# A decoder trunk on one core: MLP weights split once and kept in DRAM, relu and square through SBUF

## The chip, the core and the metric

One NeuronCore of a Trainium2 chip computes the whole layer in one launch. It has TensorE (PE, with the weight loads PEld beside it), VectorE (DVE), ScalarE (ACT), GpSimd (POOL) and SyncE (SP), which here issues every DMA. The metric is the device time of one execution in microseconds. Three runs of the kernel before took 3159.41, 3164.09 and 3166.17 us; their median, 3164.09, is the time before.

## The reference

The input x has 2048 rows of 1024 float32. One layer is computed, with a final RMSNorm:

```
h = rmsnorm(x) ; proj = h @ w_in                        # 1024 x 2700
mix = concat(stick-breaking A, sparse B, differential C, window D)   # 4 groups of 256
x = x + (mix * g_mix) @ w_out                           # 1024 x 1024
u = relu(rmsnorm(x) @ w_up)                             # 1024 x 4096
x = x + (u * u) @ w_down                                # 4096 x 1024
out = rmsnorm(x)
```

w_up and w_down hold 16.8 MB each, w_out 4.2 MB, all in float32.

## The kernel before

**Precision.** A dense product is done in fp32r in three passes: both factors are split into a high part (ACT copies the value to fp32r) and a low part (value minus high part), and high x high, high x low and low x high are added in PSUM.

**Stages.** The 2048 rows are four chunks of 512. `dense()` does the projections of all chunks (P0 to P3), then for each chunk M0 to M3 the output projection and the MLP (`mlp`). The attention scores of chunk c run beside them, so that PE, ACT and DVE serve both: the scores of the first chunk beside the projections, those of later chunks beside M0, M1 and M2. M3 needs the last chunk's attention and runs alone.

**Weights.** A weight tile is 128 partitions x 1024 float32, 524,288 bytes. A chunk of the MLP uses 72 of them: 8 of w_out, taken in pairs, 32 of w_up, taken singly, 32 of w_down, taken in pairs. `weight_specs` lists them in the order of use; in the MLP the order is up 0, up 1, then for each pair up, down, down, up. `load_weights` (line 376) brings each into one of two `raw` buffers. `split_weights` (line 390) takes one of three `w` slots (a `w_hi` and a `w_lo` buffer each), has ACT copy raw to `w_hi` and POOL or DVE subtract it into `w_lo`, and gives the raw buffer back. The subtract is POOL's two times in three; in P0 and M3 it is always DVE's. The slot is given back in `mlp` when the last product that reads it has been written down. The last entry of each MLP chunk, kind "G", is the gain of the final norm, which stays in a raw buffer until the chunk ends. Every chunk loads and splits the same 72 tiles again.

**The MLP product.** `up` forms a 128 x 512 block of the hidden layer by 24 matmuls of 512 columns; `up_end` (line 622) runs relu and square in place in PSUM on ACT, copies the result to `u_hi` on ACT and subtracts it into `u_lo` on DVE, reading PSUM. A pair of down tiles makes 48 matmuls; each result is added to `acc` by DVE. PSUM has three banks for dense products (tag pd); in M3, when attention is over, the four banks of z and t join them. At the end of a chunk ACT squares each row block of `acc` with a sum, writing the squares into the PSUM bank.

**Attention.** Rows of scores are transposed in blocks by PE, copied from PSUM to a `PT` tile by ACT, and multiplied with v. `values` (line 887) collects up to four PT tiles (RUN = 4) before `products` consumes them; there are six PT tiles (PB).

**What sets the order.** `run` holds the streams (loads, splits, finals, values, scores, fills, dense and others) in a list of fixed priority; dense comes last. It asks a planner for the time at which each stream could go on and takes the first that is ready when the planner's PE is. The planner books each operation by a cost of its own. For a DMA (`dma`, line 245), it books the bytes at 200e3 per us and at least 0.5 us, plus 2 us until the data may be used:

```
e = self.plan.op("D", [dst, src], [dst], max(n / 200e3, 0.5))
self.plan.wr[dst.tensor.name] = (e + 2.0, "D")
self.nc.sync.dma_start(dst, src)
```

The framework under it is opened with `schedule_with_timeline_sim=True` and orders each engine's instructions once more by a timeline of its own. All loads and stores stand in the one queue of SP, which waits at each until its buffer is ready.

Of the kernel before, what the change touches and what calls it, by code (L numbers as in the profile page):

```python
# [9 lines left out]
F32 = mybir.dt.float32  # L10
# [8 lines left out]
S = 2048  # L19
# [9 lines left out]
FC = 2  # L29
GPN = 3  # L30
UNITS = 4
QB, RB, PB, WB = 4, 7, 6, 3
PD, ZB, TB = 3, 2, 2
RUN = 4
GROUPS = "ACDB"
# [162 lines left out]
class Trunk:  # L198
# [4 lines left out]
    def __init__(self, ctx, tc, args):  # L203
# [21 lines left out]
                    "raw": Res(2), "nx": Res(2), "acc": Res(4), "oS": Res(3), "pc": Res(1), "unit": Res(UNITS)}  # L225
        self.constants()
        self.scratch()
        self.rawq, self.wq = [], []
        self.mix_n = [0] * NT
        self.stored = {}  # L230
        self.vq, self.fq = [], []
# [102 lines left out]
    def weight_specs(self):  # L334
# [16 lines left out]
        for kind, c in self.phases:  # L351
            if kind == "P":
                for m in ORDER[c > 0]:
                    if m in MT:
                        yield kind, c, w_in(MT[m], 0, KD)
                    else:
                        kn = WMAX // sum(w for _, w in NG[m])
                        for k0 in range(0, KD, kn):
                            yield kind, c, w_in(NG[m], k0, min(kn, KD - k0))
            else:  # L360
# [15 lines left out]
    def load_weights(self):  # L376
        for kind, c, parts in self.weight_specs():
            yield from self.res["raw"].take()
            raw = self.tile(self.dn, [128, WMAX], F32, "raw", 2)
            n = 0  # L380
# [9 lines left out]
    def split_weights(self):  # L390
        j = 0
        while True:
            while not self.rawq:
                if "raw" in self.over:
                    return
                yield None
            if self.rawq[0][0] == "G":
# [8 lines left out]
            e = self.G if (kind, c) not in (("P", 0), ("M", 3)) and j % GPN else self.V  # L406
            e.tensor_tensor(lo[:, :n], raw[:, :n], hi[:, :n].bitcast(F32), OP.subtract)
            self.res["raw"].give()
            self.wq.append((hi[:, :n], lo[:, :n]))

    def weights(self, n=1):
# [170 lines left out]
    def mlp(self, c):  # L582
# [39 lines left out]
        def up_end(ft, ps):  # L622
            self.res["w"].give()
            uh = self.tile(dn, [128, 512], F32R, "u_hi", 3)
            ul = self.tile(dn, [128, 512], F32R, "u_lo", 3)
            A.activation(ps, ps, AF.Relu)
            A.activation(ps, ps, AF.Square)
            A.activation(uh, ps, AF.Copy)
            V.tensor_tensor(ul, ps, uh.bitcast(F32), OP.subtract)
            us[ft] = (uh, ul)  # L630

        def up(ft):
# [13 lines left out]
        for fc in range(FF // 128 // FC):  # L646
# [4 lines left out]
            for i in range(4):  # L651
                ts = slice(i * 128, i * 128 + 128)
                ss = self.tile(dn, [128, 2], F32, "nt_ss", 3) if last else None
                for d in range(2):
# [6 lines left out]
                        self.res["w"].give(FC)  # L661
                    V.tensor_tensor(acc[i][:, ds_], acc[i][:, ds_], ps, OP.add)
                    if last:
                        A.activation(ps, acc[i][:, ds_], AF.Square, accum_out=ss[:, d:d + 1])
                if last:
                    V.tensor_tensor(ss[:, 0:1], ss[:, 0:1], ss[:, 1:2], OP.add)
                    r = self.rstd(dn, ss[:, 0:1], D, "nt")
# [6 lines left out]
                        self.st(dap(self.out, (c * 512 + i * 128) * D + d * 512, [[D, 128], [1, 512]]), o)  # L674
                    self.res["acc"].give()
                    if i == 3:
                        self.res["raw"].give()
# [905 lines left out]
```

## Time and profile before

| | |
|---|---|
| median of three runs | 3164.09 us (3159.41 to 3166.17) |
| profiled execution, its own time | 3159.16 us |
| its span, first to last instruction | 3157.4 us |
| PE, PEld busy | 96%, 80% |
| DVE, ACT, POOL busy | 66%, 56%, 23% |
| DMA moved | 378.09 MB, mean 120 GB/s |
| granted TensorE clock, mean | 0.989 |

Busy shares are averages over stages with different limits, so a stage is read by its own window. Matmuls are pipelined and their ends are modelled: the time from one start to the next says more than a matmul's duration. A wait is put down to the instruction that released it last.

### The profile page before, as it was taken

To read this page: it belongs to the slowest core of one execution; us is meant where nothing else is said; L and a number is where in the kernel's file an instruction comes from. 1 tells how busy PE (TensorE), PEld (TensorE's weight loads), DVE (VectorE), ACT (ScalarE), POOL (GpSimd) and SP (SyncE) were. 2 spreads that over 40 slices of the span, in tenths; PEclk is the share of its full clock that TensorE was granted. 3 is DMA by queue.
4 is the path that set the end of the run, shared out by engine and by line. 5 is a ranking of instruction groups with operands and counts; after the bars stand their busy time and mean duration, and the time that the engine had idled before them with its cause. 6 is when DMAs were issued, how large, how long until landed. Compare 5 with 4: busy or idle time off the path is not lost.

```text
span 3157.4 us, 50995 instructions
## 1 busy us (share of the span) xinstructions
PE 3027.8 (96%) x19152; PEld 2533.0 (80%) x19152; DVE 2072.5 (66%) x4278; ACT 1760.3 (56%) x3410; POOL 714.3 (23%) x479
## 2 busy tenths in 40 slices
PE   7999998999999999999999989999999999999998
PEld 6888887888887777778887777878788888788887
DVE  4774658664667887786556888788666554445545
ACT  4664667554656775555655777555555554333333
POOL 3042313332311222233211112233221112210000
PEclk9999999999999999999999999999999999999999
DMA  7678554765223324356224233453542222423332
GB/s 211 190 203 216 160 162 137 200 179 142 80 80 96 97 86 116 105 152 168 69 62 109 79 90 92 117 152 100 126 114 75 70 69 65 151 81 99 94 100 94
DMA packets 457079, 378.09 MB, mean 120 GB/s; under 512 B 127104, under 2 KB 405760, under 8 KB 455168
## 3 DMA queue, kind: packets, MB, share of 16 engines
q1 hardware_dynamic: 456832, 374.83, 42.0%
q8 instruction: 151, 2.47, 0.3%
q14 instruction: 96, 0.79, 0.1%
HBM read 321.17 MB, written 53.58 MB: 119 GB/s over the span
## 4 chain that ended last, share of the span: by engine, by line
PE 49%; DVE 10%; ACT 5%; DMA 2%; issue 2%; POOL 0%; SPq 0%; DVEq 0%; ACTq 0%; POOLq 0%
PE pdM L296 36%; DVE row L117 7%; ACT row L117 3%; PE zB L296 2%; PE tB L300 2%; PE oB L296 2%; PE zC L296 1%; DVE acc L117 1%; PE tC L300 1%; PE oC L296 1%; ACT w_hi L117 1%; PE oA L296 1%; DMA raw<-in_w_out_dram 0%; PE pdM L300 0%; DVE w_lo L117 0%
## 5 line engine op out<-in xcount | busy, mean ns | idle before, releaser
L117 POOL TENSOR_TENSOR w_lo<-raw,w_hi 128x1024 fp32r<-128x1024 f32 (+1 forms) x188 | 470.8, 2508 | 1281.1 <-ACT w_hi L117 1122.7
L117 ACT ACTIVATE w_hi<-raw 128x1024 fp32r<-128x1024 f32 (+2 forms) x376 | 389.8, 1047 | 483.7 <-PE pdM L296 280.1
L117 DVE TENSOR_TENSOR acc<-acc,pdM 128x512 f32<-128x512 f32 (+1 forms) x576 | 372.2, 653 | 198.7 <-PE pdM L296 186.0
L296 PE MATMUL pdM<-w_hi,u_hi 128*128 128x512 f32 x1024 | 410.8, 405 | 20.6 <-DVE acc L117 13.5
L296 PE MATMUL pdM<-T_hi,w_hi 128*128 128x512 f32 (+1 forms) x1088 | 415.8, 383 | 0.0
L296 PE MATMUL pdM<-T_lo,w_hi 128*128 128x512 f32 (+1 forms) x1088 | 415.0, 382 | 0.0
L296 PE MATMUL pdM<-T_hi,w_lo 128*128 128x512 f32 (+1 forms) x1088 | 414.9, 382 | 0.0
L296 PE MATMUL pdM<-w_hi,u_lo 128*128 128x512 f32 x1024 | 406.0, 396 | 5.6 <-DVE u_lo L117 5.6
L296 PE MATMUL pdM<-w_lo,u_hi 128*128 128x512 f32 x1024 | 405.2, 396 | 0.0
L117 DVE TENSOR_TENSOR w_lo<-raw,w_hi 128x1024 fp32r<-128x1024 f32 (+1 forms) x188 | 245.9, 1312 | 227.3 <-ACT w_hi L117 216.2
L117 ACT ACTIVATE row<-row 128x1024 f32<-128x1024 f32 (+7 forms) x292 | 229.1, 802 | 116.3 <-DVE row L117 114.4
L296 PEld LDWEIGHTS pdM<-w_hi,u_hi 128*128 128x128 f32 x1024 | 194.6, 190 | 66.4 <-DVE acc L117 18.7
L296 PEld LDWEIGHTS pdM<-T_hi,w_hi 128*128 128x128 f32 x1088 | 205.5, 189 | 37.0 <-issue 0.5
L296 PEld LDWEIGHTS pdM<-T_lo,w_hi 128*128 128x128 f32 x1088 | 205.4, 189 | 36.8 <-issue 0.3
L296 PEld LDWEIGHTS pdM<-T_hi,w_lo 128*128 128x128 f32 x1088 | 205.4, 189 | 36.5 <-issue 0.3
L296 PEld LDWEIGHTS pdM<-w_hi,u_lo 128*128 128x128 f32 x1024 | 195.1, 191 | 44.4 <-DVE u_lo L117 8.2
L117 ACT ACTIVATE row<-row,c_mn 128x1024 f32<-128x1024 f32 (+4 forms) x192 | 171.5, 895 | 103.9 <-DVE c_mn L117 103.2
L296 PEld LDWEIGHTS pdM<-w_lo,u_hi 128*128 128x128 f32 x1024 | 194.4, 190 | 40.7
L117 ACT ACTIVATE PT<-tB 128x512 f32<-128x512 f32 (+1 forms) x244 | 131.3, 554 | 138.0 <-PE tB L300 136.9
L296 PE MATMUL pdP<-T_lo,w_hi 128*128 128x512 f32 x480 | 190.1, 396 | 0.0
L296 PE MATMUL pdP<-T_hi,w_lo 128*128 128x512 f32 x480 | 189.3, 395 | 0.6 <-POOL w_lo L117 0.6
L296 PE MATMUL pdP<-T_hi,w_hi 128*128 128x512 f32 x480 | 189.3, 394 | 0.0
(206 smaller groups left out, 6521.7 us busy)
## 6 DMA issues: line engine op xcount, KB each, us to landing
raw<-in_w_up_dram SPq DMA_DIRECT2D x128, 512.0 KB, 4.0
raw<-in_w_down_dram SPq DMA_DIRECT2D x128, 512.0 KB, 3.5
raw<-in_w_in_dram SPq DMA_DIRECT2D x72, 512.0 KB, 5.0
acc<-in_x_dram SPq DMA_DIRECT2D x32, 512.0 KB, 4.5
raw<-in_w_out_dram SPq DMA_DIRECT2D x32, 512.0 KB, 4.8
qst<-qk_qA SPq DMA_DIRECT2D x64, 128.0 KB, 3.5
qst<-qk_qC SPq DMA_DIRECT2D x128, 64.0 KB, 3.8
qst<-qk_qD SPq DMA_DIRECT2D x64, 128.0 KB, 3.1
```

The costliest lines, as they stand in the source:

```text
L117: return f(*a, **k)
L296: self.nc.tensor.matmul(out, a, b, start=start, stop=stop, **k)
L300: self.nc.tensor.transpose(out, a, self.ident[:a.shape[0], :a.shape[0]])
```

## The change

In the first MLP chunk (c = 0) each of the 72 weight tiles is loaded and split as before, and its two parts are then stored in a DRAM tile of their own (`w_d`), 2 x 524,288 bytes. For chunks 1 to 3 `weight_specs` gives only the number of the tile (kind "S"), and `load_weights` loads both parts straight into a `w_hi` and a `w_lo` buffer. Once the raw buffers are no longer used, the two of them serve as a fourth slot (every fourth tile, `t % 4 == 0`). The final gain of these chunks takes a slot in place of a raw buffer. No splits are left in chunks 1 to 3; which engine subtracts is now decided without the exception for M3. Relu writes a float32 tile `r` in SBUF (one buffer), square works in place on it, and `u_hi` and `u_lo` are made from it; the squares at the end of a chunk go to `r` too. PT tiles go from six to five.

```
--- before.py
+++ after.py
@@ -29,7 +29,7 @@
 FC = 2
 GPN = 3
 UNITS = 4
-QB, RB, PB, WB = 4, 7, 6, 3
+QB, RB, PB, WB = 4, 7, 5, 3
 PD, ZB, TB = 3, 2, 2
 RUN = 4
 GROUPS = "ACDB"
@@ -225,7 +225,7 @@
                     "raw": Res(2), "nx": Res(2), "acc": Res(4), "oS": Res(3), "pc": Res(1), "unit": Res(UNITS)}
         self.constants()
         self.scratch()
-        self.rawq, self.wq = [], []
+        self.rawq, self.wq, self.w_d = [], [], []
         self.mix_n = [0] * NT
         self.stored = {}
         self.vq, self.fq = [], []
@@ -357,6 +357,10 @@
                         kn = WMAX // sum(w for _, w in NG[m])
                         for k0 in range(0, KD, kn):
                             yield kind, c, w_in(NG[m], k0, min(kn, KD - k0))
+            elif c:
+                for j in range(8 + 2 * FF // 128):
+                    yield "S", c, j
+                yield "G", c, [(lambda t: t, dap(self.norm_final, 0, [[0, 128], [1, D]]))]
             else:
                 for d in range(4):
                     for kk in range(2):
@@ -374,7 +378,30 @@
                 yield "G", c, [(lambda t: t, dap(self.norm_final, 0, [[0, 128], [1, D]]))]
 
     def load_weights(self):
+
+
+        t = -1
         for kind, c, parts in self.weight_specs():
+            if c and kind in "SG":
+                while t < 0 and any(x[0] not in "SG" for x in self.rawq):
+                    yield None
+                yield from self.res["w"].take()
+                if t >= 0:
+                    t += 1
+                elif self.res["raw"].free == 2:
+                    t = 0
+                tags = (("raw", 2), ("raw", 2)) if t >= 0 and t % 4 == 0 else (("w_hi", WB), ("w_lo", WB))
+                if t == 0:
+                    self.res["w"].give()
+                x = [self.tile(self.dn, [128, WMAX], F32 if kind == "G" else F32R, n, b, n) for n, b in tags]
+                if kind == "G":
+                    self.ld(x[0], parts[0][1])
+                    self.rawq.append(("G", c, x[0], 0))
+                else:
+                    for s_ in range(2):
+                        self.ld(x[s_], self.w_d[parts][128 * s_:128 * s_ + 128, :])
+                    self.rawq.append(("S", c, x, 0))
+                continue
             yield from self.res["raw"].take()
             raw = self.tile(self.dn, [128, WMAX], F32, "raw", 2)
             n = 0
@@ -394,7 +421,7 @@
                 if "raw" in self.over:
                     return
                 yield None
-            if self.rawq[0][0] == "G":
+            if self.rawq[0][0] in "GS":
                 self.wq.append(self.rawq.pop(0)[2])
                 continue
             yield from self.res["w"].take()
@@ -403,9 +430,14 @@
             lo = self.tile(self.dn, [128, WMAX], F32R, "w_lo", WB)
             j += 1
             self.A.activation(hi[:, :n], raw[:, :n], AF.Copy)
-            e = self.G if (kind, c) not in (("P", 0), ("M", 3)) and j % GPN else self.V
+            e = self.G if (kind, c) != ("P", 0) and j % GPN else self.V
             e.tensor_tensor(lo[:, :n], raw[:, :n], hi[:, :n].bitcast(F32), OP.subtract)
             self.res["raw"].give()
+            if kind == "M":
+                d = self.dram.tile([2 * 128, WMAX], F32, name=f"w_{len(self.w_d)}")
+                for s_, x in enumerate((hi, lo)):
+                    self.st(d[128 * s_:128 * s_ + 128, :], x)
+                self.w_d.append(d)
             self.wq.append((hi[:, :n], lo[:, :n]))
 
     def weights(self, n=1):
@@ -623,10 +655,11 @@
             self.res["w"].give()
             uh = self.tile(dn, [128, 512], F32R, "u_hi", 3)
             ul = self.tile(dn, [128, 512], F32R, "u_lo", 3)
-            A.activation(ps, ps, AF.Relu)
-            A.activation(ps, ps, AF.Square)
-            A.activation(uh, ps, AF.Copy)
-            V.tensor_tensor(ul, ps, uh.bitcast(F32), OP.subtract)
+            r = self.tile(dn, [128, 512], F32, "r", 1)
+            A.activation(r, ps, AF.Relu)
+            A.activation(r, r, AF.Square)
+            A.activation(uh, r, AF.Copy)
+            V.tensor_tensor(ul, r, uh.bitcast(F32), OP.subtract)
             us[ft] = (uh, ul)
 
         def up(ft):
@@ -661,7 +694,8 @@
                         self.res["w"].give(FC)
                     V.tensor_tensor(acc[i][:, ds_], acc[i][:, ds_], ps, OP.add)
                     if last:
-                        A.activation(ps, acc[i][:, ds_], AF.Square, accum_out=ss[:, d:d + 1])
+                        r = self.tile(dn, [128, 512], F32, "r", 1)
+                        A.activation(r, acc[i][:, ds_], AF.Square, accum_out=ss[:, d:d + 1])
                 if last:
                     V.tensor_tensor(ss[:, 0:1], ss[:, 0:1], ss[:, 1:2], OP.add)
                     r = self.rstd(dn, ss[:, 0:1], D, "nt")
@@ -674,7 +708,7 @@
                         self.st(dap(self.out, (c * 512 + i * 128) * D + d * 512, [[D, 128], [1, 512]]), o)
                     self.res["acc"].give()
                     if i == 3:
-                        self.res["raw"].give()
+                        self.res["w" if c else "raw"].give()
             if FC * fc + 3 < FF // 128:
                 yield from up(FC * fc + 3)
             if fc == FF // 128 // FC - 2:
```

## Rows read from the trace of the kernel before

**Rows 1.** The page, part 1: busy us, share, instructions of each engine.

```profile
PE 3027.8 (96%) x19152; PEld 2533.0 (80%) x19152; DVE 2072.5 (66%) x4278; ACT 1760.3 (56%) x3410; POOL 714.3 (23%) x479
```

**Rows 2.** Windows by stage: start:end, length, busy (count), PEclk, DMA share, GB/s.

```profile
0.00:710.00 710.00, 677.65 (x4389) 573.87 (x4389) 447.93 (x1049) 414.57 (x905) 203.90 (x175) 1.00 0.65 184
710.00:1405.00 695.00, 663.41 (x4324) 546.71 (x4321) 510.28 (x1094) 432.32 (x860) 177.55 (x105) 0.99 0.37 103
1405.00:2095.00 690.00, 661.54 (x4405) 546.43 (x4403) 495.76 (x936) 432.74 (x797) 152.75 (x85) 0.99 0.37 101
2095.00:2710.00 615.00, 601.22 (x3948) 505.06 (x3947) 388.53 (x889) 323.88 (x620) 147.98 (x86) 0.99 0.34 96
2710.00:2800.00 90.00, 75.92 (x522) 71.19 (x521) 45.65 (x74) 33.54 (x54) 25.57 (x22) 0.92 0.45 141
2800.00:3158.00 358.00, 348.07 (x1579) 289.78 (x1577) 184.32 (x239) 123.22 (x175) 6.54 (x8) 0.99 0.31 94
```

**Rows 3.** Windows of M3's start and of its steady part.

```profile
2745.00:2752.00 7.00, 3.98 (x30) 3.78 (x29) 1.95 (x3) 1.06 (x1) 0.00 (x0) 0.93 0.92 294
...
2900.00:2944.00 44.00, 44.00 (x196) 36.45 (x195) 22.60 (x29) 15.47 (x21) 0.00 (x0) 1.00 0.33 96
```

**Rows 4.** The page, part 5: the weight splits; busy us, mean ns, idle before.

```profile
L117 POOL TENSOR_TENSOR w_lo<-raw,w_hi 128x1024 fp32r<-128x1024 f32 (+1 forms) x188 | 470.8, 2508 | 1281.1 <-ACT w_hi L117 1122.7
...
L117 ACT ACTIVATE w_hi<-raw 128x1024 fp32r<-128x1024 f32 (+2 forms) x376 | 389.8, 1047 | 483.7 <-PE pdM L296 280.1
...
L117 DVE TENSOR_TENSOR w_lo<-raw,w_hi 128x1024 fp32r<-128x1024 f32 (+1 forms) x188 | 245.9, 1312 | 227.3 <-ACT w_hi L117 216.2
```

**Rows 5.** Windows of M1 and M2, instructions on tile w_hi alone.

```profile
1405.00:2095.00 690.00, 376.31 (x1276) 228.79 (x1275) 34.03 (x23) 73.86 (x71) 121.27 (x48) 0.99 0.37 101
2095.00:2710.00 615.00, 371.13 (x1283) 229.68 (x1284) 30.41 (x23) 71.95 (x69) 113.54 (x46) 0.99 0.34 96
```

**Rows 6.** Timeline of M1; tile scr (min/median/max ns); groups by line.

```profile
1463.13 2.36 POOL L117 TENSOR_TENSOR w_lo<-raw,w_hi 128x1024 fp32r<-128x1024 f32 x1 [6.92 <-ACT w_hi L117]
...
1463.80 1.97 DVE L117 CUSTOM_DVE_ANT_0 scr<-on 128x256 f32<-128x256 f32 x1
...
L117 DVE CUSTOM_DVE_ANT_0 scr<-on x48: 360/424/2624, 131.5 to 2673.5; 128x256 f32<-128x256 f32 x48
...
L117 DVE CUSTOM_DVE_ANT_0 scr<-on 128x256 f32<-128x256 f32 x48 | 38.0, 791 | 7.9 <-ACT on L117 7.4
```

**Rows 7.** Waits of PE in M3: waiting <- releaser, us, times, longest.

```profile
PE pdM L300 <- DVE nx L117: 7.0, 1, 7.0
PE pdM L296 <- ACT u_hi L117: 3.4, 1, 3.4
PE pdM L296 <- ACT w_hi L117: 3.0, 1, 3.0
```

**Rows 8.** Timeline of ACT, then the chain of waits, at M3's start.

```profile
2720.69 1.06 ACT L117 ACTIVATE w_hi<-raw 128x1024 fp32r<-128x1024 f32 x1 [1.04 <-DMA raw<-in_w_out_dram]
...
2721.65 0.58 ACT L117 ACTIVATE u_hi<-pdM 128x512 fp32r<-128x512 f32 x1
...
2744.22 5.49 DMA raw<-in_w_out_dram
...
2787.36 1.21 DVE w_lo L117
```

**Rows 9.** DMA traffic of M0 (710 to 1405 us).

```profile
DMA packets 86071, 71.70 MB, mean 103 GB/s; under 512 B 28052, under 2 KB 78484, under 8 KB 86014
```

**Rows 10.** Groups by form: relu and square, u_hi, T_hi on ACT; u_lo on DVE.

```profile
L117 ACT ACTIVATE pdM<-pdM 128x512 f32<-128x512 f32 x256 | 149.2, 583 | 12.6 <-PE pdM L296 10.1
...
L117 ACT ACTIVATE u_hi<-pdM 128x512 fp32r<-128x512 f32 x128 | 76.3, 597 | 2.6
...
L117 ACT ACTIVATE T_hi<-nx 128x512 fp32r<-128x512 f32 x64 | 39.6, 627 | 29.9 <-DVE nx L117 28.0 <-PE pdM L296 1.6
...
L117 DVE TENSOR_TENSOR u_lo<-pdM,u_hi 128x512 fp32r<-128x512 f32 x128 | 87.7, 686 | 64.5 <-ACT u_hi L117 64.2
```

More of the change, by code (lines that the diff above doesn't have):

```diff
@@ L31 @@
 UNITS = 4
-QB, RB, PB, WB = 4, 7, 6, 3
+QB, RB, PB, WB = 4, 7, 5, 3
 PD, ZB, TB = 3, 2, 2
@@ L227, in __init__ @@
         self.scratch()
-        self.rawq, self.wq = [], []
+        self.rawq, self.wq, self.w_d = [], [], []
         self.mix_n = [0] * NT
@@ L359, in weight_specs @@
                             yield kind, c, w_in(NG[m], k0, min(kn, KD - k0))
+            elif c:
+                for j in range(8 + 2 * FF // 128):
+                    yield "S", c, j
+                yield "G", c, [(lambda t: t, dap(self.norm_final, 0, [[0, 128], [1, D]]))]
             else:
@@ L376, in load_weights @@
     def load_weights(self):
+        t = -1
         for kind, c, parts in self.weight_specs():
+            if c and kind in "SG":
+                while t < 0 and any(x[0] not in "SG" for x in self.rawq):
+                    yield None
+                yield from self.res["w"].take()
+                if t >= 0:
+                    t += 1
+                elif self.res["raw"].free == 2:
+                    t = 0
+                tags = (("raw", 2), ("raw", 2)) if t >= 0 and t % 4 == 0 else (("w_hi", WB), ("w_lo", WB))
+                if t == 0:
+                    self.res["w"].give()
+                x = [self.tile(self.dn, [128, WMAX], F32 if kind == "G" else F32R, n, b, n) for n, b in tags]
+                if kind == "G":
+                    self.ld(x[0], parts[0][1])
+                    self.rawq.append(("G", c, x[0], 0))
+                else:
+                    for s_ in range(2):
+                        self.ld(x[s_], self.w_d[parts][128 * s_:128 * s_ + 128, :])
+                    self.rawq.append(("S", c, x, 0))
+                continue
             yield from self.res["raw"].take()
@@ L396, in split_weights @@
                 yield None
-            if self.rawq[0][0] == "G":
+            if self.rawq[0][0] in "GS":
                 self.wq.append(self.rawq.pop(0)[2])
@@ L405, in split_weights @@
             self.A.activation(hi[:, :n], raw[:, :n], AF.Copy)
-            e = self.G if (kind, c) not in (("P", 0), ("M", 3)) and j % GPN else self.V
+            e = self.G if (kind, c) != ("P", 0) and j % GPN else self.V
             e.tensor_tensor(lo[:, :n], raw[:, :n], hi[:, :n].bitcast(F32), OP.subtract)
             self.res["raw"].give()
+            if kind == "M":
+                d = self.dram.tile([2 * 128, WMAX], F32, name=f"w_{len(self.w_d)}")
+                for s_, x in enumerate((hi, lo)):
+                    self.st(d[128 * s_:128 * s_ + 128, :], x)
+                self.w_d.append(d)
             self.wq.append((hi[:, :n], lo[:, :n]))
@@ L625, in up_end @@
             ul = self.tile(dn, [128, 512], F32R, "u_lo", 3)
[L626 to L629, printed above, removed]
+            r = self.tile(dn, [128, 512], F32, "r", 1)
+            A.activation(r, ps, AF.Relu)
+            A.activation(r, r, AF.Square)
+            A.activation(uh, r, AF.Copy)
+            V.tensor_tensor(ul, r, uh.bitcast(F32), OP.subtract)
             us[ft] = (uh, ul)
@@ L663, in mlp @@
                     if last:
-                        A.activation(ps, acc[i][:, ds_], AF.Square, accum_out=ss[:, d:d + 1])
+                        r = self.tile(dn, [128, 512], F32, "r", 1)
+                        A.activation(r, acc[i][:, ds_], AF.Square, accum_out=ss[:, d:d + 1])
                 if last:
@@ L676, in mlp @@
                     if i == 3:
-                        self.res["raw"].give()
+                        self.res["w" if c else "raw"].give()
             if FC * fc + 3 < FF // 128:
```

## The prediction

> **What bounds the kernel now.** I began with the page's busy shares: PE 96%, DVE 66%, ACT 56%, POOL 23% [rows 1]. A busy PE is not a PE at its peak, so next I cut the span into stages with the view of windows [rows 2]. The cuts are where the PSUM tiles of the projections end (710 us) and where each MLP chunk M0 to M3 begins (710, 1405, 2095, 2710); beside M0 to M2 run the scores of the later attention chunks, and M3 runs alone. PE's idle time, window less busy, is 32 us in the projections, 32 in M0, 28.5 in M1, 13.8 in M2, 14.1 in the first 90 us of M3 and 9.9 in the rest of it, the tail included: 130 us in all. In M3's steady part PE issues 196 matmuls in 44 us, 224 ns each, without a gap [rows 3]. So the matmuls set the time, and nothing the change does removes one. What it can win is idle time, and only where the weight splits stand in the way. The idle share goes with the load of the two helpers: DVE 73% and ACT 62% in M0 with 4.5% idle, 72% and 63% in M1 with 4.1%, 63% and 53% in M2 with 2.2%.
>
> **What goes.** Before, all 72 weight tiles of each MLP chunk are split: one ACT copy and one subtract, on POOL twice in three and on DVE else (M3: DVE always) [rows 4]. In M1 this is 73.9 us of ACT, 34.0 of DVE and 121.3 of POOL, in M2 72.0, 30.4 and 113.5 [rows 5]. All of it goes in chunks 1 to 3, and M0 and the projections keep theirs.
>
> A POOL split also costs DVE: a 256-wide sum of squares that takes 0.42 us in the median took 1.97 us while a POOL split ran, and its 48 calls average 791 ns, 17.7 us above 48 medians [rows 6]. A quarter of all POOL splits are M1's, so this form alone gives back some 4.5 us there; with the other forms that read two SBUF tiles I take 10 us of DVE in M1 and 9 in M2 (4.5 from the row is the low end).
>
> M1's load falls to ACT (432.7 - 73.9)/690 = 52% and DVE (495.8 - 34.0 - 10)/690 = 65%. That is what M2 runs at now, with 2.2% idle: 15.5 us in place of 28.5, a gain of 13. M2 falls to 41% and 57%, between its present row and M3's steady part (34% and 51%, idle only in the tail); I halve its 13.8 us, a gain of 7. Together 20 us. The bounds: nothing, if the planner, which gives attention the first claim, spends the freed time on bringing attention forward at the same density, so that each score waits as before; and 42 us, if all idle time of M1 and M2 goes.
>
> In M3 PE hides nearly all splits already, so 72 splits less give nothing but at the start. There three waits are named [rows 7]. 3.4 us for u_hi: the ACT queue holds a w_hi copy at 2720.7 ahead of u_hi at 2721.7 [rows 8]. 3.0 us for w_hi itself, after a w_out load that took 5.5 us to land. 7.0 us for the norm chain, with one DVE split of 1.21 us in it [rows 8]. Removed: 3.4 + 3.0 + 1.2 = 7.6 us. What is late next is the second w_out tile. Before, two raw and three split buffers let two w_out tiles come in ahead; now the four slots hold the last two w_down tiles, the final gain and one w_out tile, and the second w_out load waits until the last down product has let its slot go. By the 5.5 us landing and 1.8 us for its second half (524 KB at the 294 GB/s of [rows 3]), less 12 matmuls of the first tile (about 0.12 us each for 256 columns, half of 224 ns), it is up to 5.9 us late; nothing, if other rows' first halves go in between. I take 4. M3: -3.6 us.
>
> **What is added.** M0 stores each split tile: 72 tiles of two 524 KB parts, 75.5 MB, on the SP queue. A store waits for the same subtract for which the next raw load waits already, so SP stands no longer than before; behind it in the queue are the attention's loads and that raw load, which lands later by the time of 1.05 MB, 3.6 us at 294 GB/s, against a weight tile every 695/72 = 9.7 us. The traffic goes from 71.7 MB [rows 9] to 147 MB in 695 us, 212 GB/s. The nearest row is the projections' own stage: 184 GB/s, DMA share 0.65, and 4.6% idle, M0's own share. By it the cost is nothing. The other end is in the planner: the kernel's dma() books every transfer at 200 KB per us, so M0's bookings go from 359 us to 736 us, more than the 695 us of the stage. Bookings are no durations, but they order the streams: products would be placed as if weights and keys came late. If the stage stretched to its bookings it would cost 41 us. I take 8, near the row.
>
> M1 to M3 load 1.05 MB per tile in place of 0.52. In M1 and M2 the traffic becomes some 155 GB/s, under the projections' 184. In M3 the tight place is a pair of w_down tiles, 2.1 MB, asked for when the pair before is done and needed two up tiles (48 x 224 ns = 10.8 us) later: 7.1 us at 294 GB/s and under 2 us to start. Hidden, with some 2 us to spare. If that cover goes, a rival below has the price.
>
> PB falls from 6 to 5. A run holds four PT tiles and one more is taken before the run is flushed, so five are in use at most; only a copy that the scheduler pulled ahead of a flush loses its place. From 0 to 5 us; I take 1.
>
> Relu and square through SBUF: PSUM to PSUM took 583 ns, PSUM to SBUF 597, SBUF to SBUF 627 [rows 10], so a tile's three steps go from 583 + 583 + 597 to 597 + 627 + 627, 88 ns more, 128 times: 11 us of ACT, 2.8 in each chunk, less than a twentieth of what ACT is freed of in M1 to M3. The PSUM bank comes free after the relu. From -5 us (the few waits of products for a bank) to +4; I take +1. The Trainium skill, "ScalarE: Activation LUTs", Step-by-step: what each stage is for, speaks against this edit: given the choice, ACT should write to PSUM, its nearer port. The rows agree in sign; by the rule alone the edit would be a loss and nothing else, the 11 us of ACT above.
>
> The subtract u_lo now reads two SBUF tiles where one was PSUM (686 ns, [rows 10]). The split row of [rows 6] shows what POOL can do to such an operation; in M0 POOL is busy 26% of the time, so 32 x 0.26 x about 1.5 us, 12 us of DVE in M0 at most, beside PE's work and inside the 8 us above. The Trainium skill, "SBUF — State Buffer", section "SBUF: two separate sides", says that a DVE operation with two SBUF inputs and a GpSimd operation lock each other out for a whole instruction. By that rule u_lo is newly exposed in M0 and free in M1 to M3, where POOL has little left but the norms.
>
> **The sum.** -20 - 3.6 + 8 + 1 + 1 = -13.6 us. On the profiled execution (3159.16 us, span 3157.4) that is 3145.6. The median of the runs, 3164.09, is 4.9 us above that execution, so I forecast 3150.
>
> **Rivals.**
> - The freed time moves nothing: PE is at 96%, attention is only brought forward and waits as densely as before. M1 and M2 give 0 to 5 us, M3 3.6, M0 costs 4 to 8: 3160 to 3168, say 3164. For it: the stall of M1 is mostly DVE row work of attention, which stays. Against it: M2's row, half the idle share at a lower load. Chance 0.24.
> - M0 runs to its bookings (slower): the order written at 736 us of transfers starves dense products of weights and attention of keys, M0 grows by 41 us, the gains of 23.6 and the small costs of 2 stay: 3164 + 41 - 24 + 2 = 3183. It decides from where PE's idle time in M0 grows past 32 + 24 us. For it: booked time above the stage. Against it: the row of the projections. Chance 0.15.
> - Weights late in M3 (slower): if a pair comes at the projections' 184 GB/s and not 294, 2.1 MB take 11.4 + 1.7 = 13.1 us against 10.8, 2.3 us for each of 15 pairs, 35 us: 3164 + 35 - 14 = 3185. Against it: M3 has the DMA engines to itself, with a share of 0.31 now. Chance 0.07.
> - The forecast: 0.54, its own range 3132 to 3162.
>
> **How the numbers follow.** The range goes from 3122 (all 42 us of M1 and M2 gone) to 3182, into the slower rivals. About 0.2%, 6.3 us, is what a measurement tells from no change: faster means under 3157.8, slower over 3170.4. Most of the forecast's 0.54 and a little of the first rival are faster: 0.53. The middle of the first rival and the forecast's upper edge: 0.25. Both slower rivals: 0.22.
>
> **What would show it.** Windows of M1 and M2 with ACT some 10 points lower and PE idle near 15 and 7 us in stages of about the same work; M0's idle time under 45 us with a DMA share near 0.7; no DVE sum of squares over 1 us after M0; M3's steady part still 224 ns for each matmul, with no PE wait on a w_hi load; at M3's start a wait for a w_out load in place of those for ACT. I am wrong if the idle time of M1 and M2 stays above 35 us together, if M0's passes 56 us, or if PE waits for weights in M3's pairs.

## The result, and the profile after

The changed kernel takes 3130.41 us (3127.61 to 3133.62) against 3164.09 (3159.41 to 3166.17): ratio 0.989 with a 95% interval of 0.988 to 0.991, 33.7 us faster. The forecast was 3150. The direction was right, and less than half of the gain was foreseen; the time lies just under the forecast's own range of 3132 to 3162. Its profiled execution took 3130.41 us, its span is 3128.7; against the 3157.4 of before that is 28.7 us. The other 5.0 us are the choice of the execution: the one profiled before was 4.9 us under its median, this one is at its median.

Part 1 of the page after, against [rows 1]:

```profile
PE 3026.6 (97%) x19152; PEld 2531.7 (81%) x19152; DVE 1861.2 (59%) x4158; ACT 1565.4 (50%) x3194; POOL 468.6 (15%) x383
```

PE is busy for the same time, within 1.2 us, so in these two traces nearly all that was won is idle time of PE. The three helpers lost 211, 195 and 246 us.

The windows of [rows 2] were cut at round times. To compare the kernels stage by stage I cut both at the first w_out product of each chunk. Columns: start:end, length, busy and count of PE, PEld, DVE, ACT, POOL, PEclk, DMA share, GB/s. Before, M0 to M3:

```profile
718.50:1401.50 683.00, 656.28 (x4274) 540.67 (x4272) 501.78 (x1078) 425.32 (x844) 174.42 (x104) 0.99 0.37 102
1401.50:2111.20 709.70, 678.91 (x4496) 560.15 (x4496) 514.82 (x979) 447.79 (x830) 160.99 (x92) 0.99 0.37 103
2111.20:2733.50 622.30, 606.32 (x3959) 509.53 (x3960) 384.40 (x870) 323.74 (x616) 151.72 (x87) 0.99 0.34 96
2733.50:3157.40 423.90, 404.57 (x2013) 345.39 (x2011) 218.55 (x296) 145.35 (x209) 20.13 (x21) 0.98 0.34 103
```

After, M0 to M3, and the steady part of M3 of [rows 3]:

```profile
722.20:1383.40 661.20, 644.85 (x4186) 531.34 (x4185) 480.36 (x1025) 411.12 (x811) 158.47 (x94) 0.99 0.66 215
1383.40:2079.10 695.70, 673.98 (x4516) 559.65 (x4515) 450.09 (x969) 386.96 (x767) 46.04 (x50) 1.00 0.50 160
2079.10:2706.40 627.30, 618.26 (x4024) 515.65 (x4023) 340.33 (x882) 268.55 (x562) 34.49 (x42) 0.99 0.47 157
2706.40:3128.70 422.30, 405.47 (x2021) 345.07 (x2018) 139.00 (x228) 80.06 (x142) 19.04 (x21) 0.99 0.53 191
2900.00:2944.00 44.00, 44.00 (x196) 36.45 (x195) 13.41 (x20) 7.45 (x12) 0.00 (x0) 1.00 0.53 191
```

PE's idle time is length less busy: 26.7, 30.8, 16.0 and 19.3 us before, 16.4, 21.7, 9.0 and 16.8 after; the projections went from 36.8 to 38.2. The stages are not equal pieces of work (the planner moved some attention from M0 into M1 and M2, see the counts), so the lengths can't be compared one by one, but idle time can. In M3's steady part nothing moved: 196 matmuls in 44 us, now with DMA at 191 GB/s instead of 96.

The groups that answer to [rows 4], [rows 6] and [rows 10], of the kernel after (busy us, mean ns | idle before):

```profile
L117 POOL TENSOR_TENSOR w_lo<-raw,w_hi 128x1024 fp32r<-128x1024 f32 x86 | 218.0, 2537 | 542.9 <-ACT w_hi L117 430.8 <-PE pdM L296 25.8 <-DMA qst<-qk_qC 20.7
L117 DVE TENSOR_TENSOR u_lo<-r,u_hi 128x512 fp32r<-128x512 f32 x128 | 91.9, 718 | 254.6 <-ACT u_hi L117 254.6
L117 DVE TENSOR_TENSOR w_lo<-raw,w_hi 128x1024 fp32r<-128x1024 f32 x62 | 81.7, 1318 | 75.6 <-ACT w_hi L117 68.7 <-PE pdP L296 5.0 <-DMA kst<-qk_kC 1.1
L117 ACT ACTIVATE r<-r 128x512 f32<-128x512 f32 x128 | 80.7, 630 | 2.6
L117 ACT ACTIVATE u_hi<-r 128x512 fp32r<-128x512 f32 x128 | 80.7, 630 | 2.8
L117 ACT ACTIVATE r<-pdM 128x512 f32<-128x512 f32 x128 | 75.8, 592 | 325.4 <-PE pdM L296 317.5 <-DVE u_lo L117 7.7
L117 DVE CUSTOM_DVE_ANT_0 scr<-on 128x256 f32<-128x256 f32 x48 | 27.4, 571 | 9.6 <-ACT on L117 9.1
```

Relu, square and copy cost nearly what the forecast said (592 + 630 + 630 ns a block against 597 + 627 + 627). The sum of squares came down from 791 to 571 ns. The waits of PE from 2660 us on, against [rows 7] (us, times, longest):

```profile
PE pdM L296 <- DMA w_hi<-w: 2.6, 1, 2.6
PE pdM L296 <- ACT u_hi L117: 1.6, 1, 1.6
PE pdM L296 <- POOL T_lo L117: 1.4, 2, 1.0
...
PE pdM L296 <- DMA w_lo<-w: 0.7, 1, 0.7
...
PE pdM L300 <- DVE nx L117: 0.6, 1, 0.6
```

The wait for ACT's w_hi copy is gone, that for the norm chain went from 7.0 to 0.6 us, and the load of a w_out tile is late once, 2.6 + 0.7 us, as foreseen. M0's traffic, against [rows 9], doubled:

```profile
DMA packets 99227, 142.45 MB, mean 215 GB/s; under 512 B 25194, under 2 KB 73962, under 8 KB 99169
```

### The profile page after: what moved, and what is told of

Same layout as the page of the kernel before. It is cut to its first block, busy times and chain, and to the rows that moved or that the text cites. A ratio compares the mean times of both kernels' runs of the same rounds, so it can differ in the third digit from the quotient of the medians.

```text
span 3128.7 us, 51197 instructions
## 1 busy us (share of the span) xinstructions
PE 3026.6 (97%) x19152; PEld 2531.7 (81%) x19152; DVE 1861.2 (59%) x4158; ACT 1565.4 (50%) x3194; POOL 468.6 (15%) x383
## 4 chain that ended last, share of the span: by engine, by line
PE 77%; DVE 9%; ACT 6%; DMA 4%; issue 2%; SPq 1%; POOL 0%; DVEq 0%; POOLq 0%; ACTq 0%
PE pdM L296 43%; PE pdP L296 13%; DVE row L117 7%; ACT row L117 4%; PE zB L296 4%; PE tB L300 4%; PE oB L296 4%; PE zC L296 2%; PE oC L296 2%; PE tC L300 2%; DVE acc L117 1%; DMA raw<-in_w_in_dram 1%; PE zA L296 1%; PE zD L296 1%; PE tA L300 1%
## 5 line engine op out<-in xcount | busy, mean ns | idle before, releaser
L296 PE MATMUL pdM<-T_hi,w_lo 128*128 128x512 f32 (+1 forms) x936 | 358.5, 383 | 0.0
L296 PE MATMUL pdM<-w_hi,u_hi 128*128 128x512 f32 x776 | 312.1, 404 | 13.0 <-DVE acc L117 6.8
L117 POOL TENSOR_TENSOR w_lo<-raw,w_hi 128x1024 fp32r<-128x1024 f32 (+2 forms) x92 | 229.0, 2492 | 570.8 <-ACT w_hi L117 458.7
L296 PE MATMUL pdM<-w_hi,u_lo 128*128 128x512 f32 x776 | 306.5, 395 | 2.5 <-DVE u_lo L117 2.5
L296 PE MATMUL pdM<-w_lo,u_hi 128*128 128x512 f32 x776 | 306.7, 395 | 0.0
L117 DVE TENSOR_TENSOR u_lo<-r,u_hi 128x512 fp32r<-128x512 f32 x128 | 91.9, 718 | 254.6 <-ACT u_hi L117 254.6
L117 ACT ACTIVATE r<-pdM 128x512 f32<-128x512 f32 x128 | 75.8, 592 | 325.4 <-PE pdM L296 317.5
L117 ACT ACTIVATE w_hi<-raw 128x1024 fp32r<-128x1024 f32 (+2 forms) x160 | 164.5, 1035 | 118.6 <-DMA raw<-in_w_in_dram 53.4
L117 ACT ACTIVATE row<-row,b_mw 128x640 f32<-128x640 f32 (+7 forms) x160 | 134.5, 842 | 119.3 <-DVE b_mw L117 118.5
L296 PE MATMUL pdM<-raw,u_hi 128*128 128x512 f32 x496 | 189.8, 391 | 0.0
```

The costliest lines, as they stand in the source:

```text
L117: return f(*a, **k)
L296: self.nc.tensor.matmul(out, a, b, start=start, stop=stop, **k)
```

## The experiments

The ratio is always to the kernel before, run beside it; that one's median in these comparisons was 3161.2 to 3163.5 us. The edits are shown in excerpts; a first line in brackets names the kernel that is edited where it is not the one before and the text doesn't name it, and three dots stand for lines left out.

**First question: which part of the change moves the time?** The relu tile and the five PT tiles alone, in the kernel before (label r_only):

```diff
-QB, RB, PB, WB = 4, 7, 6, 3
+QB, RB, PB, WB = 4, 7, 5, 3
-A.activation(ps, ps, AF.Relu)
-A.activation(ps, ps, AF.Square)
+r = self.tile(dn, [128, 512], F32, "r", 1)
+A.activation(r, ps, AF.Relu)
+A.activation(r, r, AF.Square)
```

> The kernel before with the SBUF tile r and five PT tiles alone; no weight is stored, all chunks split theirs. Relief theory (the gain is what ACT, DVE and POOL no longer do in M1 to M3): 3164 us, within 5, PE idle in M0 near the 27 us of before. Bank theory (the PSUM bank that comes free after the relu shortens waits in every chunk, and so in M0): 3154 or less, PE idle in M0 near 16 us. Order theory (the planner's bookings for the stores changed the order in M0): 3164, as the relief theory.

Measured: 3152.33 us, 0.9965 [0.9953, 0.9978]. About 9 us faster; what that is worth shows below (hop16).

The opposite, the change without the relu tile, five PT tiles kept (w_only):

```diff
 (the kernel after)
-r = self.tile(dn, [128, 512], F32, "r", 1)
-A.activation(r, ps, AF.Relu)
-A.activation(r, r, AF.Square)
+A.activation(ps, ps, AF.Relu)
+A.activation(ps, ps, AF.Square)
```

> The changed kernel with relu, square and the final squares in PSUM again (PT tiles stay at five): the weights' part alone. Relief theory: 3130 us, within 5. Bank theory: 3140 or more, M0's idle time back near 27 us. Order theory: 3130, within 5.

Measured: 3130.20 us, 0.990 [0.9886, 0.9913]: what the whole change gives. So beside the stored weights the relu tile is worth nothing either way, and the bank theory, which had 3140 or more here, falls.

All of the change, but chunks 1 to 3 go on loading and splitting the raw weights, and M0's 75 MB of stores are never read (stores_only):

```diff
 (the kernel after)
-elif c:
-    for j in range(8 + 2 * FF // 128):
-        yield "S", c, j
...
-if kind == "M":
+if (kind, c) == ("M", 0):
     d = self.dram.tile(...)
```

> The changed kernel whose chunks 1 to 3 load and split their weights as before: M0 stores 75 MB that nobody reads. Relief theory: no gain left, 3164 to 3172 us, M0's idle time 27 us or more. Bank theory: some 3154, M0 near 16 us. Order theory: some 3154, M0 near 16 us. My forecast's term for the stores, +8 us, would show here as M0 longer than with r alone.

Measured: 3149.62 us, 0.9962 [0.9949, 0.9976], 2.7 us under r_only. The window of M0 in r_only, then in stores_only:

```profile
717.30:1385.80 668.50, 646.41 (x4202) 531.59 (x4201) 487.00 (x1040) 415.51 (x819) 165.74 (x101) 0.99 0.37 103
718.40:1380.20 661.80, 644.93 (x4182) 530.73 (x4180) 480.00 (x1021) 411.45 (x811) 159.72 (x94) 0.99 0.65 214
```

With the stores the DMA share is 0.65 in place of 0.37, and PE is idle for 16.9 us in place of 22.1 (26.7 in the kernel before). The stores cost nothing that can be seen.

**Second: do the bookings of the stores cost anything?** The 144 stores are issued without a booking in the planner (unbooked):

```diff
 (the kernel after)
-self.st(d[128 * s_:128 * s_ + 128, :], x)
+self.nc.sync.dma_start(d[128 * s_:128 * s_ + 128, :], x.bitcast(F32))
```

> The changed kernel whose 144 stores are issued without being booked in the planner; the transfers are the same. Relief and bank theories: 3130 us, within 5. Order theory: M0 loses its gain, 3138 to 3145, idle there near 27 us.

Measured: 3122.70 us, 0.9871 [0.9857, 0.9884], 7.7 us under the kernel after. Its M0:

```profile
718.70:1387.40 668.70, 646.34 (x4203) 532.71 (x4201) 484.56 (x1030) 413.64 (x816) 157.89 (x97) 0.99 0.65 214
```

M0's idle time is 22.4 us, 6.0 more than after's 16.4 and about r_only's 22.1 without any store. So the 7.7 us do not come from M0, and booked stores go with less idle time there, not more. The mean granted clock is higher. After, then unbooked (span, clock):

```profile
core 0: 3128.7 us, clock 0.991
```

```profile
core 0: 3115.6 us, clock 0.994
```

PE's busy time is 3007.6 us for the same 19152 matmuls, 19.0 less. The granted clock has two levels, 2.4 and 1.2 GHz, and the traces show 59 us of the span at the lower one in after and 36 in unbooked, 23 apart. At the lower level PE does little more than half the work: in the kernel before, matmuls of 256 columns start every 0.21 us from 719 to 722 us, where the granted clock is 0.50, and every 0.12 us from 724 us on, where it is 1.00. So some 10 of the 19 us are, by this estimate, the clock's. The order of the work changed, and the rest of what changed in it I can't name.

All transfers booked at double speed, in the kernel before (before_400) and in the one after (after_400):

```diff
-e = self.plan.op("D", [dst, src], [dst], max(n / 200e3, 0.5))
+e = self.plan.op("D", [dst, src], [dst], max(n / 400e3, 0.5))
```

> The kernel before with transfers booked at 400 KB per us. If the bookings at 200 hold back the order in general: 3150 or less, as the changed kernel gained 12. If they hurt only where M0's stores and the double loads fill them: 3150 to 3165, no more than the scatter of the order.

> The changed kernel whose planner books transfers at 400 KB per us in place of 200. Order theory, as the run without bookings for the stores points: 3123 us or less, fewer stretches at the half clock. Relief theory: 3130, within 4.

Measured: 3163.70 us, 1.0008 [1.0000, 1.0017] in the kernel before; 3118.14, 0.9857 [0.9842, 0.9872] in the one after. Bookings do not hold the kernel before. With the stores, less booked time goes with 8 to 12 us less.

**Third: how much does an order alone scatter?** One constant of the planner is changed by a fifteenth, no work is touched, in the kernel before (hop16) and after (after_hop16):

```diff
-HOP, MARGIN = 0.15, 0.1
+HOP, MARGIN = 0.16, 0.1
```

> The kernel before with one planner constant moved (the booked time from engine to engine 0.16 us in place of 0.15): no work changes, the order does. If order by itself moves little (relief theory): 3162 us, within 4. If the order of the streams moves the time by as much as the part with r alone did (order theory): anything from 3150 to 3174.

> The changed kernel with the planner's booked hop at 0.16 us in place of 0.15: the order alone moves. If order scatters the changed kernel as it did the one before (3161 to 3150): anywhere from 3118 to 3142. If the gain of the change is its relief alone: 3130, within 4.

Measured: 3149.64 us, 0.9960 [0.9947, 0.9973] for the kernel before, 11.8 us faster for nothing; 3121.28, 0.9872 [0.9860, 0.9885] for the one after, 9.1 faster. So a single order is a draw, and two orders of the same work can differ by some 10 us, a scatter that repeated runs of one kernel don't show: the intervals of these ratios are 0.0013 to either side, 4 us. The 9 us of r_only and the 8 to 12 of the bookings can't be told from a draw. Every edit that follows draws a new order too.

**Fourth: what in the splits costs?** The copies are kept and the subtracts go: M0 stores the raw tile in place of the high part, and ACT makes the high part in place in chunks 1 to 3 (copy_kept):

```diff
 (the kernel after)
-for s_, x in enumerate((hi, lo)):
+for s_, x in enumerate((raw, lo)):
...
+if kind == "S":
+    self.A.activation(x[0], x[0].bitcast(F32), AF.Copy)
```

> The changed kernel, but M0 stores the unsplit tile in place of the high part, and in M1 to M3 ACT copies it to fp32r in place (one ACT copy for each of 216 tiles, as before); the low part comes ready. DMA bytes as in the changed kernel. If ACT's freed time carries the gain: back to 3145 or more, M1's idle time 27 us or more. If DVE and POOL carry it (the lock and the subtracts): 3130 to 3137. My forecast gave each about half: 3140.

Measured: 3141.68 us, 0.9934 [0.9921, 0.9947], 11.3 over the kernel after, no more than two orders can differ by.

The subtracts are kept and the copies go: M0 stores the raw tile in place of the low part, and POOL (two in three) or DVE subtracts in place in chunks 1 to 3 (sub_kept):

```diff
 (the kernel after)
-for s_, x in enumerate((hi, lo)):
+for s_, x in enumerate((hi, raw)):
...
+if kind == "S":
+    j += 1
+    e = self.G if j % GPN else self.V
+    e.tensor_tensor(x[1], x[1].bitcast(F32), x[0].bitcast(F32), OP.subtract)
```

> The changed kernel, but M0 stores the unsplit tile in place of the low part, and in M1 to M3 POOL (two in three) or DVE subtracts the high part from it in place; ACT copies nothing. If DVE and POOL carry the gain: back to 3145 or more, with DVE sums of squares of some 2 us in M1 again. If ACT carries it: 3130 to 3137.

Measured: 3169.86 us, 1.0021 [1.0010, 1.0032], 39.4 over the kernel after and slower than before. The subtracts are the dear part. Two things in these runs are not as in the kernel before: in both, M0 gives the raw buffer back only behind its store, and in sub_kept POOL subtracts in M3 too, which was DVE's there. What POOL's work costs by itself the next run asks. It is w_only with work for POOL that nobody needs or waits for: for two of three tiles of chunks 1 to 3, POOL reads the two parts and writes their sum to a spare tile (dummy_pool).

```diff
 (w_only)
+if j % GPN:
+    for h in range(2):
+        d = self.tile(self.dn, [128, 512], F32, "r", 1)
+        self.G.tensor_tensor(d, *[t[:, 512 * h:512 * h + 512].bitcast(F32) for t in x], OP.add)
```

> The run with the weights' part alone (3130 us, relu and square in PSUM), with two POOL additions of 512 columns for two of three tiles of chunks 1 to 3, which read the tile's two parts when they have landed and write a spare tile; no product waits for them, and ACT and DVE get no work. Lock theory (what left DVE free in M1 and M2 is POOL's reading, not the splits' own work): DVE's sums of squares take 2 us again beside POOL, DVE is some 50 us busier in M1 and M2 together, 3148 us or more. Own-work theory (ACT copies and DVE subtracts were the load): 3130 to 3136.

Measured: 3153.54 us, 0.9973 [0.9963, 0.9982], 23.3 over w_only. Part 1 of the page of w_only, then of dummy_pool:

```profile
PE 3021.9 (97%) x19152; PEld 2529.2 (81%) x19152; DVE 1850.0 (59%) x4158; ACT 1557.3 (50%) x3194; POOL 473.6 (15%) x383
```

```profile
PE 3032.8 (96%) x19152; PEld 2536.9 (80%) x19152; DVE 1891.4 (60%) x4158; ACT 1555.4 (49%) x3194; POOL 860.9 (27%) x671
```

DVE runs the same 4158 instructions and is busy 41.4 us longer: its own instructions became longer beside POOL's. A second effect is mixed in. DVE also waits for POOL's part of the norms, which stands behind the adds in POOL's queue. Waits in M1 and M2, of w_only and then of dummy_pool (us, times, longest):

```profile
DVE on L117 <- POOL gn_rs L117: 7.4, 12, 0.7
DVE onC L117 <- POOL gc_rs L117: 3.2, 6, 1.0
```

```profile
DVE on L117 <- POOL gn_rs L117: 17.1, 14, 5.1
DVE onC L117 <- POOL gc_rs L117: 13.4, 7, 5.8
```

That is 20 us more of waiting. In the kernel before no wait of this kind is longer than 1.6 us. So the 23.3 us are the price of POOL's work as such, not of the lengthening alone, and they hold a new order as well: of the 24.3 us between the two spans, 10.9 are busy time of PE and 13.4 its idle time, 16.5 more in M1 and M2 and 3.1 less elsewhere.

**Fifth: POOL out of the way without a stored weight.** All subtracts of weights go to DVE, in the kernel before (before_dve), after (after_dve) and after_400 (after_400_dve):

```diff
-GPN = 3
+GPN = 1
```

> The kernel before with every split's subtract on DVE (GPN = 1) and nothing stored: it takes some 188 x 2.5 us off POOL and adds 188 x 1.23 = 231 us to DVE, and takes away about 200 us that DVE's operations run over their medians. Lock theory: DVE's load about even and shorter waits, 3125 to 3150, so part of the change's gain is to be had without storing a weight. Own-work theory: DVE has 30 us more in each of M1 and M2, 3165 or more.

> The changed kernel with the remaining subtracts of the projections and M0 on DVE, bookings as they are. Lock theory: 25 to 40 us under the changed kernel, 3090 to 3105, as the run with both edits points. If that run's gain came from the bookings and DVE together only: 3110 to 3130. Its distance to the kernel before with DVE alone is what storing the weights is worth where POOL stands in nobody's way: own work of 216 copies and 216 subtracts.

> The changed kernel with bookings at 400 KB per us and every remaining subtract (projections and M0) on DVE. That adds some 92 x 1.23 = 113 us of DVE work and takes away what POOL's reading costs DVE there (about 110 us above the medians in the changed kernel's trace). Lock theory: about even, 3110 to 3122, with idle time in the projections and M0 no higher. Own-work theory: slower, 3125 or more.

Measured: before_dve 3108.62 us, 0.9827 [0.9813, 0.9840]; after_dve 3093.91, 0.9783 [0.9770, 0.9796]; after_400_dve 3086.66, 0.9763 [0.9750, 0.9775]. The first and the last came out faster than either theory said, which had 3125 and 3110 at the least. One constant in the old kernel beats the whole change by 21.8 us, and the two together are the best version: 74.5 us under the kernel before. Page part 1 and three groups of before_dve:

```profile
PE 3004.5 (97%) x19152; PEld 2528.8 (82%) x19152; DVE 2108.7 (68%) x4466; ACT 1766.1 (57%) x3410; POOL 250.7 (8%) x291
```

```profile
L117 DVE TENSOR_TENSOR w_lo<-raw,w_hi 128x1024 fp32r<-128x1024 f32 x364 | 447.6, 1238 | 315.3 <-ACT w_hi L117 307.8 <-PE pdM L296 3.0 <-DMA qk_qC<-u_lo 1.8
...
L117 DVE CUSTOM_DVE_ANT_0 scr<-on 128x256 f32<-128x256 f32 x48 | 21.2, 441 | 3.4 <-ACT on L117 2.9
...
L117 DVE CUSTOM_DVE_ANT_0 scr<-onC 128x64 f32<-128x64 f32 x64 | 15.8, 248 | 4.0 <-ACT onC L117 3.2
```

DVE took over 188 splits, 188 x 1.24 = 233 us by their mean here, and its busy time rose by 36.2 us only. The other 197 us are what POOL's 188 splits had cost DVE, 1.05 us a split. As the records of neighbouring instructions overlap, that is a little high: added up record by record, what DVE's instructions beside a POOL split took over the median of their form in before_dve and after_dve is 175 us, 0.93 a split. A rival is that PE waited for POOL's splits themselves, 2.5 us long where DVE's take 1.24. In the kernel before PE's waits that a POOL instruction ended last are 0.6 us in all; those that DVE ended went from 68.3 us to 48.6 in before_dve, those that ACT ended from 38.8 to 26.6. (In hop16, where no work changes, they are 51.3 and 44.5, so a part of the first drop can be the order's.) Between before_dve and after_dve, where POOL is in neither's way, storing the weights is worth 14.7 us: that is the price of the splits' own work, with the scatter of two orders in it.

Last, the subtracts T_lo of the activations go from POOL to DVE as well (all_dve, from after_400_dve):

```diff
-self.G.tensor_tensor(lo, r, hi.bitcast(F32), OP.subtract)
+self.V.tensor_tensor(lo, r, hi.bitcast(F32), OP.subtract)
```

> The changed kernel with bookings at 400 KB per us and all subtracts on DVE, those of the transposed rows (T_lo) too, which POOL did in 1.42 us each and DVE does in some 0.69: 96 x 0.69 = 66 us more DVE work. Lock theory: 3070 to 3085, and the wait for T_lo at M3's start gone. Own-work theory: 3088 to 3095.

Measured: 3095.05 us, 0.9790 [0.9777, 0.9803], 8.4 over after_400_dve, where 3070 to 3085 was expected. A miss. Page part 1 of after_400_dve, then of all_dve:

```profile
PE 3000.7 (97%) x19152; PEld 2526.9 (82%) x19152; DVE 1864.1 (60%) x4250; ACT 1569.2 (51%) x3194; POOL 237.5 (8%) x291
```

```profile
PE 3007.6 (97%) x19152; PEld 2533.6 (82%) x19152; DVE 1888.4 (61%) x4346; ACT 1568.0 (51%) x3194; POOL 112.6 (4%) x195
```

The 96 subtracts cost DVE only 24.3 us of busy time, 96 x 0.68 = 65 for themselves less 41 by which other instructions became shorter (33 if the records are added up), and POOL is 124.9 us less busy. PE's idle time grew by 12.2 us (span less busy: 81.2 to 93.4), 8.6 of it in M0. The two executions profiled lie 19.1 us apart in span, the medians 8.4. Whether the loss is DVE's extra load or one more draw of the order is open.

## Why the prediction was wrong in size

The ledger of PE's idle time by stage, in us. The last two columns are means over five orders each: the kernel before, hop16, before_400, r_only and stores_only (none of which has the weights ready), and the kernel after, after_hop16, after_400, unbooked and w_only (all of which have).

| | forecast | before to after | five before | five after |
|---|---|---|---|---|
| projections | 0 | +1.4 | 36.4 | 37.8 |
| M0 | +8 | -10.4 | 23.5 | 20.2 |
| M1 and M2 | -20 | -16.0 | 43.6 | 29.9 |
| M3 | -3.6 | -2.5 | 18.4 | 16.0 |
| PB, relu tile | +2 | (in the stages) | | |
| PE busy | 0 | -1.2 | 3029.8 | 3017.3 |
| sum of the changes | -13.6 | -28.7 | | -30.5 |

**The step that failed is M0's: the 8 us taken for the stores' bookings are not there, and M0 gained instead.** The prediction said that bookings "order the streams" and took 8 us for it. In the two traces M0 gave back 10.4 us, 18.4 away from that; the other terms together were 3.3 us too hopeful. The stores themselves cost nothing: unbooked, with 75 MB of them at 0.65 DMA share, has M0 idle for 22.4 us, and r_only, without any, for 22.1. The row of the projections that the prediction named as the nearest (4.6% idle at 0.65) was the one to take, at its word: nothing. The bookings went with less idle time: 16.9 us in stores_only against 22.1 in r_only, 16.4 in the kernel after against 22.4 in unbooked. All runs with POOL's splits fall in two groups by this. Where M0 has stores booked at 200 KB per us (the kernel after, w_only, stores_only, after_hop16, copy_kept, sub_kept, dummy_pool), it is idle for 15.5 to 19.2 us; where it has no stores, or theirs unbooked or booked at half (the kernel before, r_only, hop16, before_400, unbooked, after_400), for 22.1 to 29.0. (In the ledger stores_only stands among the five before, though its M0 is that of the kernel after.) Several of these orders are much alike in M0, so they are fewer draws than runs. By the two pairs above some 5 to 6 of the 10.4 us go with the bookings, and the rest, from the kernel before to r_only, can't be told from a draw. How booked time shortens PE's waits in M0 is not shown, and it doesn't decide the kernel's time: unbooked and after_400, with more idle time in M0, are faster as a whole. With all subtracts on DVE the groups don't hold (9.1 us in before_dve without stores, 11.5 in after_dve with them).

**M1 and M2** were forecast well in time: -20, measured -16.0 in the pair, -13.8 over the five orders, which don't overlap here (40.1 to 46.8 us without the weights ready, 21.7 to 33.9 with). That is partly luck, as two sizes inside the term were off and worked against each other. ACT fell less than said, from 63% to 56% of M1 where 52% was forecast, and from 52% to 43% of M2 where 41% was. The relief of DVE from POOL's lengthening was taken as 19 us and was three to four times that. DVE's busy time fell by 211.3 us [rows 1], of which its own splits are 245.9 - 87.1 = 158.8 (62 of 1024 columns above and six narrower ones, 87.1 us in all), and u_lo gave 4.2 back, so some 57 us are other instructions that became shorter, with their number unchanged. Added up record by record, DVE's instructions in M1 and M2 stood 88 us over the medians of their forms before and 15 after. I had priced it by one form's mean; the other forms were priced by guess. DVE time is no bound, and PE's idle time fell by less than DVE's. By cause, about half of the gain is the splits' own work (14.7 us, after_dve against before_dve; the ACT copies alone 11.3, copy_kept) and the rest of the 31 to 34 us is, by subtraction, POOL out of the way; dummy_pool prices that at 23.3, by itself and with a longer queue. Each of these figures holds a scatter of some 10 us, so the halves are an estimate and not shown.

**What the sum had no term for.** PE's busy time was taken as fixed ("the matmuls set the time"). Within the pair it was; over the five orders it fell by 12.4 us. The traces show where most of that is. The granted clock is at its lower level, 1.2 GHz, in 9 to 16 stretches of each of the ten traces, and but for the last one, the tail of the kernel, each of them begins in a wait of PE or close behind one: in the kernel before PE waits 4.2 us for DVE until 717.1 us, and from 717 to 722 us the clock is 0.50. The stretches add up to 69 us on the mean of the five orders before and 49 of the five after; 19 us in which matmuls start every 0.21 us in place of 0.12 are some 8 us of PE's time. So a wait that goes can give back more than its own length. And the 4.9 us between the profiled execution and the median were carried forward, where the kernel after has no such gap.

**M3** came out near the number, -2.5 against -3.6, and that is partly luck, as the named waits don't match one by one: the norm chain gave 6.4 us where 1.2 were taken, and new short waits for T_lo and T_hi came in its place; a w_out load is late by 3.3 where 4 were taken. The rival of late weights fell: 224 ns a matmul, no wait for a weight in the steady part. The rival in which M0 runs to its bookings fell: 16.4 us idle, under the 56 from which it was to decide. The rival in which the freed time moves nothing fell too: the idle share of M1 went from 4.3% to 3.1%, that of M2 from 2.6% to 1.4%.

**The relu tile**: 88 ns a block more were forecast, and the rows show (592 + 630 + 630) - (583 + 583 + 597) = 89. No time hangs on it (w_only 3130.20, after 3130.41). The Trainium skill, "ScalarE: Activation LUTs", Step-by-step: what each stage is for, prefers PSUM as ACT's target; the rows agree in sign, and the kernel's time does not show it. u_lo, now with two SBUF inputs, rose from 686 to 718 ns in the mean, 4 us in all, and to 818 in sub_kept, where POOL is at work in all chunks. Its median hardly moved (685 to 692 ns); its longest call went from 0.69 to 2.78 us.

**The sums of squares on DVE.** The prediction said that none over 1 us would be left after M0. Two are (1.36 us at 1487.9, 1.34 at 2148.1), each beside a T_lo subtract of POOL. Before there were nine, eight of them beside a w_lo split, up to 2.62 us.

**Open.** How the 31 to 34 us divide between the splits' own work, the lengthening of DVE and POOL's queue can't be read finer than some 10 us, since each edit draws a new order. Why orders differ in idle time was not pursued.

## What to carry to other kernels

Before removing work from a busy helper, ask what that work does to its neighbours: here the POOL subtracts took about 1 us apiece from DVE, and moving them onto the busier DVE (one constant, 0.983) won more than storing 75 MB of ready weights (0.989). Price a shared resource by adding up all instructions that get longer, not by one form. Where a planner writes the order, change one of its constants that touches no work, and take the scatter that this gives as the smallest difference that a part of an edit can be credited with.

## What the runs showed of the hardware

A DVE instruction that reads only SBUF can become longer while POOL runs a subtract or add over SBUF tiles; one that reads a PSUM tile, alone or beside an SBUF tile, does not. In the kernel before 284 DVE instructions that read only SBUF overlap a POOL subtract, and 146 of them took over 0.2 us more than the median of their form in before_dve and after_dve; of 340 that read PSUM none took over 0.02 us more. The tile scr in the kernel before (min/median/max ns, first and last start):

```profile
L117 DVE CUSTOM_DVE_ANT_0 scr<-on x48: 360/424/2624, 131.5 to 2673.5; 128x256 f32<-128x256 f32 x48
L117 DVE TENSOR_TENSOR scr<-tB,b_cf x32: 397/424/425, 348.8 to 2672.6; 128x256 f32<-128x256 f32 x32
L117 DVE TENSOR_TENSOR on<-on,scr x32: 394/424/2228, 349.5 to 2673.1; 128x256 f32<-128x256 f32 x32
```

The same in before_dve:

```profile
L117 DVE CUSTOM_DVE_ANT_0 scr<-on x48: 364/420/1544, 131.1 to 2632.7; 128x256 f32<-128x256 f32 x48
L117 DVE TENSOR_TENSOR scr<-tB,b_cf x32: 397/420/426, 345.7 to 2631.3; 128x256 f32<-128x256 f32 x32
L117 DVE TENSOR_TENSOR on<-on,scr x32: 397/424/425, 347.1 to 2631.8; 128x256 f32<-128x256 f32 x32
```

tB is in PSUM: the group that reads it never passes 426 ns, with POOL's splits or without. on and scr are in SBUF: their product takes up to 2.23 us with POOL's weight splits about and 0.43 without them. The sum of squares of on is left with one long call in before_dve, 1.54 us at 541.7, beside a T_lo subtract. The Trainium skill, "SBUF — State Buffer", SBUF: two separate sides, says that a DVE operation with two SBUF inputs and a GpSimd operation that reads SBUF hold the shared port for a whole instruction and block the other; the maxima here agree.

The same subtract of 128 x 1024 float32 took 2.5 us on POOL and 1.24 on DVE; of 128 x 512, 1.3 to 1.5 on POOL and 0.68 on DVE (T_lo in all_dve). And loads of 4 KB rows at 191 GB/s beside products without a gap cost PE nothing in M3.
